# A decoder layer with seven-product projections: loads and operand splits moved to other places, row loads tied behind operand loads, the first MLP block loaded apart

## The chip, the cores and the metric

The kernel runs on one core of a Trainium2 chip. The metric is the device time of one execution in microseconds (us), and the median of several runs is compared. The core has five engines that the profile names: PE (TensorE, the matmuls, with PEld for its weight loads), DVE (VectorE), ACT (ScalarE), POOL (GpSimd) and SP (SyncE, which here only issues DMAs). ACT and POOL issue DMAs too, each in its own queue, between their other instructions.

## The reference

One decoder layer over 1024 tokens of width 1024, all in float32:

```python
u = x * (1.0 + sc1) + sh1
proj = u @ w_in
y_a = _sliding_window_attention(qa, ka, va, sinks) @ w_oa
y_b = _gated_deltanet(dq, dk, dv, z, b_raw, a_raw, ...) @ w_ob
mixed = (sigmoid(g_a) * y_a + sigmoid(g_b) * y_b) @ w_out
x = _layer_norm(ALPHA * x + (1.0 + gt1) * mixed, ln1_g, ln1_b)
u2 = x * (1.0 + sc2) + sh2
h = square(relu(u2 @ w_ff1 + b_ff1))
x = _layer_norm(ALPHA * x + (1.0 + gt2) * (h @ w_ff2 + b_ff2), ln2_g, ln2_b)
```

The shifts, scales and gates (`sh1`, `sc1`, `gt1` and so on) come from a small product of the conditioning vector with `w_ada`. `w_ff1` is 1024 x 4096 and `w_ff2` 4096 x 1024.

## The kernel before

**Operands.** Each float32 operand of a large product is split into a high part (a copy on ACT, line 212) and a low part (a subtraction on DVE, line 213), and each product is made of three matmuls: high by high, high by low, low by high. `split_s` issues the ACT copy at once and the DVE subtraction some places later.

**Seven products.** The projections `w_oa`, `w_ob`, `w_ff1` and `w_ff2` are each done as a 2 x 2 block product in seven block products instead of eight, so that sums and differences of blocks are operands. Their names in the code are 11, 21, 22, T1, T2, T3 and T4; m is the number of the product.

**Order by hand.** PE, DVE and ACT run in an order that is written out. `count` is the number of matmuls issued so far, and `at(p, f)` lets `f` issue its instructions when `count` reaches p; p is called a place here. Since each engine runs its own list in order, a place fixes only which instruction stands before which on one engine: an engine may run ahead of PE, and stands where an instruction of its own must wait. DMAs that ACT issues stand in its list as well (`ga_load`, `ta_load`, `sg_load`). SP and POOL are not ordered by hand: a planner orders their DMAs, and each goes out when the buffer it writes is free and its data is there.

**Stages from 915 us on**, where the change lies:

- OA is the place of the first output projection (`y_a`, stage 0 in the loop whose matmul is line 1684), OB = OA + 336 that of the second (`y_b`, stage 1). Each has two groups of 168 places, 12 places to a product. In one part of a group, products 1, 6, 7 and 4 add into the same PSUM bank one after the other, and between two of them the bank is read: by a copy on ACT (`o_part`, line 1614) or by an add on DVE (`o_full`, line 1433). In the other part, products 5 and 3 share a bank in the same way. The first product 1 of stage 1 stands at OB+72 and 84 (two column blocks), product 6 at OB+96 and 108; the adds between are placed at OB+85 and 97.
- The operands of stage 0 are partly in SBUF (11, T2, T3, T4 are split by `q_part`) and partly loaded: `q_load` and `q2_load` bring T1, 21, 22 and then all seven of stage 1 into the three `or` buffers, and `q_split` and `q2_split` split them at the places in `RSPLIT` and `RSPLIT2`, two halves to a name. A load is let go by the low part of the split three halves before it. The first three go out at `CLOSE` = OA+26, when the memory of the stage before is free, whose last user is `gz`, the evacuation of the last gate unit, and its DMA to `gb_d` (lines 1396 and 1397). Weights for the products are loaded as `owr` and split as `wo`.
- `ga_load` and `ga_act` load and squash the gates of `y_a`, `ta_load` loads the gated `y_a` back in stage 1, `sg_load` and `sg_act` (line 1633) do the same for the gates of `y_b`; `o_gate` (line 1618) writes the gated `y_a` to `ta_d`, and `y_out` (lines 1637, 1638) forms the sum. `ga` and `ta` share two `gate` buffers.
- `hd_out` writes the last head's output; its inner `more` makes the negative (`neg`, line 1373), writes it to DRAM and lets POOL add it into the stored sums T2, T3 and T4 by accumulating DMAs.
- E0 = OB + 336 begins the mix (`w_out`, line 1900), four segments of SEG = 96 places, with the layer norm and its transposes between (`u2_turn`, line 1771, `pair_turn`, line 1820, `t_split`). Its weights and the first five blocks of `w_ff1` come through the two `wr` buffers (`w_go`, `w_more`); `w_first` splits the first block, `W0`, at E0+330.
- F0 = E0 + 384 begins the first MLP matmul (line 2271; `f_load`, `f_beta`, `f_gamma`), G0 the last product (line 2331). There `s_load` brings two operands of 512 KB for every 24 places, the first two steps from ACT's queue, the rest from SP's. `rows_load` brings six row vectors, each spread over all 128 partitions (512 KB), placed at G0+62 and every 24 places after; `rr_load` brings the residual, placed at G0+200 and every 60.

Of the kernel before, what the change touches and what calls it, by code (L numbers as in the profile page):

```python
# [9 lines left out]
F32 = mybir.dt.float32  # L10
F32R = mybir.dt.float32r
# [23 lines left out]
def hybrid_layer_kernel(ctx: ExitStack, tc: tile.TileContext,  # L35
# [122 lines left out]
    for q in (0, 1, 0):  # L158
        for kq in range(4):
            later.append((w_out[kq * Q:(kq + 1) * Q, q * HALF:(q + 1) * HALF].rearrange("(k p) c -> p k c", p=P),  # L160
                         [P, 2, HALF]))
    later += [in_cols(w_ff1, i * P) for i in range(EARLY)]
    ready, raws = [], []
    AHEAD = 2

# [1191 lines left out]
    def hd_out(h, half):  # L1357
        d = heads[h]
        assert ("o", h) in flags
        tp = psum("b", 2)  # L1360
        for j in range(4):
            T.transpose(tp[:, chunk(j)], o_chunk(d, 4 * half + j), ident)

        def put():
            V.scalar_tensor_tensor(out=d["sz"][:, halves[half]], in0=tp, scalar=normw, in1=d["sz"][:, halves[half]],
                                   op0=ALU.mult, op1=ALU.mult)
            r, k, o = d["sz"][:, halves[half]], h % 4, oq_d
            if h == 7 and half == 0:
                d["vr"] = gpool.tile([P, S], F32, tag="gate", name="neg")
            neg = d["vr"][:, halves[half]]  # L1370

            def more():
                A.activation(out=neg, in_=r, func=AF.Copy, scale=-1.0)
                if h < 4 and half == 1:
                    nc.sync.dma_start(out=o["T3"][k], in_=neg)
                    for name, src in (("T1", neg), ("T4", neg), ("T2", d["vr"][:, halves[0]])):
                        nc.gpsimd.dma_start(out=o[name][k], in_=src, accum_op=ALU.add)
                elif h >= 4:
                    if h == 7:
                        nc.sync.dma_start(out=nq_d[half], in_=neg)  # L1380
                    src = nq_d[half] if h == 7 else neg
                    for name, src in ((("T4", src),), (("T3", o["22"][k]), ("T2", src), ("T4", o["22"][k])))[half]:
                        nc.gpsimd.dma_start(out=o[name][k], in_=src, accum_op=ALU.add, max_dma_last_dim=HALF)

            for name in (("11", "T1", "T4"), ("T2",))[half] if h < 4 else (("21", "22")[half],):
                nc.sync.dma_start(out=o[name][k], in_=r)
            act(4, 2.7, more)
        now("V", 2, 3.3, put)

    def gb_done(i):  # L1390
# [125 lines left out]

    REST = [(n, j) for n in ("T1", "21", "22") for j in range(2)]
    OB = OA + 336
    RSPLIT = (70, 76, 94, 100, 116, 124)
    ORDER2 = ("11", "T1", "21", "22", "T2", "T3", "T4")  # L1520
    HOME2 = {"11": (1, 6), "21": (1, 0), "T1": (1, 2), "22": (1, 4), "T2": (0, 0), "T3": (0, 2), "T4": (0, 4)}
    REST2 = [(n, j) for n in ORDER2 for j in range(2)]
    RSPLIT2 = (150, 160, 196, 206, 220, 230, 316, 340, 348, 358, 372, 384, 398, 412)

    for kind, h in units_h:
        if kind == "q":
# [123 lines left out]
        after(6, lambda: V.scalar_tensor_tensor(out=lo, in0=y, scalar=-1.0, in1=hi.bitcast(F32),  # L1650
                                                op0=ALU.mult, op1=ALU.subtract))

    for p, q, g, c in ((30, 80, 0, 3), (60, 100, 0, 0), (136, 166, 0, 2), (160, 190, 0, 1), (190, 226, 1, 0),
                       (210, 246, 1, 1), (278, 306, 1, 3), (302, 332, 1, 2)):
        at(OA + p, ga_load, g, c)
        at(OA + q, ga_act, g, c)
    for p, g, c in ((-8, 0, 0), (18, 0, 1), (108, 0, 3), (134, 0, 2), (190, 1, 2), (192, 1, 0), (275, 1, 3), (322, 1, 1)):
        at(OB + p, ta_load, g, c)
    for p, q, f in ((10, 50, 0), (12, 62, 1), (14, 90, 4), (16, 100, 5), (200, 240, 6), (202, 248, 7), (204, 260, 2), (206, 270, 3)):
        at(OB + p, sg_load, f)  # L1660
        at(OB + q, sg_act, f)
    for p, f, half in ((218, 0, None), (224, 1, None), (258, 6, 0), (266, 4, None), (274, 5, None), (290, 7, 0),
# [139 lines left out]
    def u2_rest(j, p):  # L1802

        at(p, t_one, j)
        at(p + 1, quad_split, j, "22", 1, 1)
        at(p + 8, t_sums, j)
        for kh in range(2):
            for k in range(4):
                at(p + 12 + 3 * (4 * kh + k), t_split, j, kh, k)

    rawp = {}

# [67 lines left out]

    W0 = []

    def w_first():
        raw = raws.pop(0)[0]
        for kh in range(2):
            W0.append([pe.tile([P, 4, P], F32R, tag="t", name="w0", bufs=8) for _ in "hl"])
            split_s(W0[kh][0], W0[kh][1], raw[:, 4 * kh:4 * kh + 4, :], 5)

    w_more()
    for p in [1, 13] + [SEG * s + o for s in (0, 2) for o in (61, 73, 86, 98)] + [3 * SEG + o for o in (42, 98, 118, 134, 154)]:  # L1890
        at(E0 + p, w_first if p == 3 * SEG + 42 else w_go)
        at(E0 + p + 8, w_more)

    def mix_mm(pt, tok, c):

# [155 lines left out]
    at(F0 + 1, f_load, 0)  # L2051
    at(F0 + 32, f_sums, 0, V)
    at(F0 + 33, f_sums2, 0, V)
    at(F0 + 92, f_beta, 0)
    at(F0 + 100, f_gamma, 0)
    at(pos[0, 5] + 10, f_delta, 0)
    for i in range(1, NPAIR):
        if i < EARLY:
# [69 lines left out]
    def s_load(s):  # L2128
# [7 lines left out]
            src = w_ff2[(r0 + f) * P:(r0 + f + 2) * P, halves[c0]].rearrange("(f p) c -> p f c", p=P)  # L2136
        else:
            src = wt_d[{5: 0, 6: 1, 7: 2, 4: 3}[m], f:f + 2].rearrange("f p c -> p f c")
        q.dma_start(out=b, in_=src)

    def s_split(s, j):
        hi, lo = stp[s, j] = [s_tile(w, F32R, "sp") for w in PARTS[place(s)][2 * j:2 * j + 2]]
# [13 lines left out]
    def rows_load(n):  # L2156
        name, src = ROWS[n]
        rows_[name] = wp.tile([P, D], F32, tag="wl" if n % 2 else "wh", name=name)
        row(rows_[name], src, nc.sync)

    def rows_sums():
        G2, B2 = rows_["G2"], rows_["B2"]
# [3 lines left out]

    def rr_load(t):
        rr[t] = big.tile([P, D], F32, tag=f"{'hl'[t // 4]}{4 + t % 4}", name="rr")
        nc.sync.dma_start(out=rr[t], in_=res_d[SLOTS[t]])

    def res_sums(t, i):
        r = rr[t]
# [237 lines left out]
```

## Time and profile before

| | |
|---|---|
| median of three runs | 1798.21 us (1798.05 to 1801.23) |
| the profiled execution | 1799.15 us |
| its span, first to last instruction | 1797.4 us |
| mean granted TensorE clock | 0.997 |

The span by stage, with what PE and the DMA engines did:

| stage | span, us | PE busy, us | DMA share | GB/s |
|---|---|---|---|---|
| all before the projections | 0 to 915 | 909.41 | 0.74 | 198 |
| first output projection | 915 to 996 | 78.17 | 0.97 | 316 |
| second output projection | 996 to 1079 | 78.66 | 0.64 | 225 |
| mix | 1079 to 1174 | 93.61 | 0.43 | 149 |
| first MLP matmul | 1174 to 1482 | 307.52 | 0.82 | 279 |
| last product | 1482 to 1797 | 305.96 | 0.63 | 216 |

How to read the rows that follow: a row of a timeline has the start and the length in us, the engine (with q: its sequencer, which issues a DMA), the line, the operation, what it writes and reads, the shape and the count; in square brackets stands how long the engine was idle before it and what ended that. PE's matmuls are pipelined, so that a matmul is shown longer than the distance to the next one.

### The profile page before, as it was taken

How to read it: one execution, taken by the hardware profiler on the slowest of the kernel's cores; microseconds unless marked ns; L12 is line 12 of the kernel's file. 1: busy time of each engine (PE TensorE's matmuls, PEld its weight loads, DVE VectorE, ACT ScalarE, POOL GpSimd, SP SyncE). 2: the span in 40 equal slices, each digit the busy share in tenths (PEclk: the TensorE clock that was granted, in tenths of full speed). 3: DMA queues.
4: the chain of work that ended last, by engine and by line, in shares of the span. 5: the costliest groups of instructions: out<-in, count | busy, mean ns of one | idle time of the engine just before them, and what ended most of it. 6: DMA issues, size and time to landing. Idle time of an engine off the chain costs nothing.

```text
span 1797.4 us, 26402 instructions
## 1 busy us (share of the span) xinstructions
PE 1773.3 (99%) x9086; PEld 1491.4 (83%) x9086; DVE 1316.5 (73%) x2391; ACT 1055.7 (59%) x2373; POOL 367.6 (20%) x495
## 2 busy tenths in 40 slices
PE   9999999999999999999999999999999999999998
PEld 6888888888888888888887788788888888888887
DVE  7689588988855576766657666888777765676697
ACT  4689578887874565665565542475555554434341
POOL 0334235665531011122111000002122210000000
PEclk9999999999999999999999999999999999999999
DMA  9557945687786687877889754369888889655671
GB/s 330 163 204 266 287 141 133 119 182 133 144 243 197 154 211 212 222 210 200 237 236 342 271 188 164 129 190 320 306 276 272 285 296 384 228 196 182 207 258 48
DMA packets 287305, 393.85 MB, mean 219 GB/s; under 512 B 27994, under 2 KB 180259, under 8 KB 286915
## 3 DMA queue, kind: packets, MB, share of 16 engines
q1 hardware_dynamic: 219282, 245.95, 42.6%
q0 software_dynamic: 51856, 112.62, 24.3%
q10 hardware_dynamic: 16032, 33.59, 5.3%
q8 instruction: 72, 1.18, 0.3%
q14 instruction: 63, 0.51, 0.1%
HBM read 273.86 MB, written 141.83 MB: 231 GB/s over the span
## 4 chain that ended last, share of the span: by engine, by line
PE 83%; DMA 5%; DVE 5%; ACT 3%; issue 1%; POOL 0%; ACTq 0%; DVEq 0%; SPq 0%; POOLq 0%
PE mm L255 30%; PE mm L2271 8%; PE mm L2331 6%; PE a L2331 4%; PE b L2331 4%; PE b L2271 4%; PE mm L1684 4%; PE a L2271 3%; PE c L2331 2%; PE c L939 2%; PE mm L183 1%; PE mm L185 1%; PE mm L184 1%; PE b L1684 1%; PE a L864 1%
## 5 line engine op out<-in xcount | busy, mean ns | idle before, releaser
L255 PE MATMUL mm<-uh,wh 128*128 128x512 f32 x800 | 319.6, 400 | 0.0
L255 PE MATMUL mm<-uh,wl 128*128 128x512 f32 x800 | 319.4, 399 | 0.0
L255 PE MATMUL mm<-ul,wh 128*128 128x512 f32 x800 | 318.8, 398 | 0.0
L213 DVE TENSOR_TENSOR sp<-sraw,sp 128x1024 fp32r<-128x1024 f32 x112 | 132.7, 1220 | 77.0 <-ACT sp L212 77.0
L212 ACT ACTIVATE sp<-sraw 128x1024 fp32r<-128x1024 f32 x112 | 112.6, 1054 | 121.9 <-PE b L2331 75.3
L255 PEld LDWEIGHTS mm<-uh,wh 128*128 128x128 f32 x800 | 150.7, 188 | 26.2
L255 PEld LDWEIGHTS mm<-uh,wl 128*128 128x128 f32 x800 | 150.8, 189 | 26.1
L255 PEld LDWEIGHTS mm<-ul,wh 128*128 128x128 f32 x800 | 150.8, 188 | 26.1
L2331 PE MATMUL mm<-sp 128*128 128x512 f32 x528 | 136.2, 389 | 1.0 <-DVE sp L213 1.0
L2331 PEld LDWEIGHTS mm<-sp 128*128 128x128 f32 x528 | 98.7, 188 | 21.7 <-DVE sp L213 1.5
L2331 PE MATMUL a<-sp 128*128 128x512 f32 x336 | 92.3, 389 | 0.0
L1309 ACT ACTIVATE vn<-a,brk 128x128 f32<-128x128 f32 x64 | 23.6, 369 | 110.4 <-PE a L1307 110.4
L1684 PE MATMUL mm<-qh,wo 128*128 128x512 f32 x256 | 81.3, 395 | 4.9 <-ACT sg L1633 4.3
L871 DVE CUSTOM_DVE_ANT_0 nscore<-a,amask,nsink 128x256 f32<-128x256 f32 (+1 forms) x128 | 54.4, 462 | 40.8 <-PE a L864 40.5
L2331 PE MATMUL b<-sp 128*128 128x512 f32 (+1 forms) x336 | 79.7, 374 | 0.0
L882 POOL TENSOR_TENSOR sm<-sm 128x256 f32<-128x256 f32 x56 | 56.6, 1011 | 93.7 <-ACT sm L878 68.3
L2331 PEld LDWEIGHTS a<-sp 128*128 128x128 f32 x336 | 63.1, 188 | 13.1
L2331 PEld LDWEIGHTS b<-sp 128*128 128x128 f32 x336 | 60.3, 188 | 11.2
L230 DVE TENSOR_TENSOR wl<-wr,wh 128x1024 fp32r<-128x1024 f32 x48 | 62.7, 1306 | 6.1 <-ACT wh L226 5.9
L213 DVE TENSOR_TENSOR wl<-fraw,wh 128x1024 fp32r<-128x1024 f32 x43 | 52.5, 1221 | 15.9 <-ACT wh L212 15.9
L212 ACT ACTIVATE wh<-fraw 128x1024 fp32r<-128x1024 f32 x43 | 45.0, 1056 | 32.0 <-PE b L2271 27.0
L1684 PEld LDWEIGHTS mm<-qh,wo 128*128 128x128 f32 x256 | 48.9, 191 | 16.4 <-ACT sg L1633 4.7
(562 smaller groups left out, 4782.8 us busy)
## 6 DMA issues: line engine op xcount, KB each, us to landing
wr<-in_w_in_dram SPq DMA_DIRECT2D x60, 512.0 KB, 4.6
sraw<-hf_d SPq DMA_DIRECT2D x54, 512.0 KB, 4.4
adaw<-in_w_ada_dram SPq DMA_DIRECT2D x83, 256.0 KB, 5.1
fraw<-in_w_ff_dram SPq DMA_DIRECT2D x32, 512.0 KB, 5.7
sraw<-wt_d SPq DMA_DIRECT2D x32, 512.0 KB, 4.3
hf_d<-t ACTq DMA_DIRECT2D x48, 256.0 KB, 5.2
wt_d<-wx POOLq DMA_DIRECT2D x48, 256.0 KB, 3.1
sraw<-in_w_ff_dram SPq DMA_DIRECT2D x22, 512.0 KB, 5.4
```

The costliest lines, as they stand in the source:

```text
L183: T.matmul(t, lhsT=wh[:, k, :], rhs=xh[k][:, sl], start=k == 0, stop=False)
L212: A.activation(out=hi, in_=src, func=AF.Copy)
L213: after(lag, lambda: V.tensor_tensor(out=lo, in0=src, in1=hi.bitcast(F32), op=ALU.subtract))
L230: V.tensor_tensor(out=hl[1], in0=raw, in1=hl[0].bitcast(F32), op=ALU.subtract)
L255: T.matmul(ts[half], lhsT=w[:, k, :], rhs=xx[k][:, sl], start=k == 0 and m == 0, stop=k == KT - 1 and m == 2)
L871: V.tensor_tensor_reduce(out=ns[:, i, 1:1 + W], in0=sc[:, i * 2 * P:i * 2 * P + W], in1=amask[:, mo:mo + W], scale=-1.0, scalar=nsink[:, 2 ...
L882: behind["join"] = G.tensor_tensor(out=sm[:, :, 1 + P:1 + 2 * P], in0=sm[:, :, 1:1 + P], in1=sm[:, :, 1 + P:1 + 2 * P], op=ALU.add).ins
L939: T.matmul(av[:, 0:256], lhsT=vt[:, b, :], rhs=p_[:, m, :], start=p_ is full and m == 0, stop=p_ is prods[-1][1] and m == 1)
L1309: after(1, lambda: A.activation(out=vn, in_=Wp[:, 0:P], func=AF.Copy, scale=brk[:, n, h:h + 1]))
L1684: T.matmul(pt, lhsT=lw[:, k, own], rhs=r[:, k % 2, :], start=begin and k == 0 and x_ == 0, stop=k == 3 and x_ == 2, skip_group_check=True)
L2271: T.matmul(pt, lhsT=a[:, kk, :], rhs=b[k], start=begin and k == 0 and x_ == 0, stop=k == 3 and x_ == 2, skip_group_check=True)
L2331: T.matmul(to, lhsT=a[:, f, t * P:(t + 1) * P], rhs=b[:, f, lo:up], start=(begin or own) and s % NS == 0 and f == 0 and x_ == 0, stop=s % ...
```

## The change

It has five parts. (1) In `hd_out`, for the last head, `more` goes to OA+28 and OA+34 instead of the place right behind its source. (2) In the two output projections, the places of the operand splits (`RSPLIT`, `RSPLIT2`) and of the loads and sigmoids of `ga`, `ta` and `sg` are other ones. (3) The first block of `w_ff1` no longer goes through the `wr` buffers but is loaded in two halves into tiles of its own (tag `t`, which the mix's evacuation uses too) at E0+254 and 258 and split at E0+310 and 314; `t_split` comes six places later. (4) `f_beta` and `f_gamma` of the first pair go from F0+92 and 100 to 78 and 97. (5) In the last product, each `rows_load` and `rr_load` is tied on SP's queue behind the last `s_load` placed before it. What is computed does not change.

```diff
-    later += [in_cols(w_ff1, i * P) for i in range(EARLY)]
+    later += [in_cols(w_ff1, i * P) for i in range(1, EARLY)]
...
-            act(4, 2.7, more)
+            if h == 7:
+                at(OA + (28, 34)[half], more)
+            else:
+                act(4, 2.7, more)
...
-    RSPLIT = (70, 76, 94, 100, 116, 124)
+    RSPLIT = (62, 68, 86, 100, 112, 126)
...
-    RSPLIT2 = (150, 160, 196, 206, 220, 230, 316, 340, 348, 358, 372, 384, 398, 412)
+    RSPLIT2 = (150, 160, 196, 206, 220, 230, 262, 286, 316, 328, 344, 356, 372, 388)
...
-    for p, q, g, c in ((30, 80, 0, 3), (60, 100, 0, 0), (136, 166, 0, 2), (160, 190, 0, 1), (190, 226, 1, 0),
+    for p, q, g, c in ((50, 92, 0, 3), (75, 108, 0, 0), (136, 166, 0, 2), (160, 190, 0, 1), (190, 226, 1, 0),
                        (210, 246, 1, 1), (278, 306, 1, 3), (302, 332, 1, 2)):
         at(OA + p, ga_load, g, c)
         at(OA + q, ga_act, g, c)
-    for p, g, c in ((-8, 0, 0), (18, 0, 1), (108, 0, 3), (134, 0, 2), (190, 1, 2), (192, 1, 0), (275, 1, 3), (322, 1, 1)):
+    for p, g, c in ((36, 0, 0), (60, 0, 1), (108, 0, 3), (134, 0, 2), (190, 1, 2), (192, 1, 0), (275, 1, 3), (322, 1, 1)):
         at(OB + p, ta_load, g, c)
-    for p, q, f in ((10, 50, 0), (12, 62, 1), (14, 90, 4), (16, 100, 5), (200, 240, 6), (202, 248, 7), (204, 260, 2), (206, 270, 3)):
+    for p, q, f in ((10, 52, 0), (24, 66, 1), (72, 120, 4), (86, 132, 5), (200, 240, 6), (206, 248, 7), (218, 262, 2), (228, 274, 3)):
         at(OB + p, sg_load, f)
         at(OB + q, sg_act, f)
...
-                at(p + 12 + 3 * (4 * kh + k), t_split, j, kh, k)
+                at(p + 18 + 3 * (4 * kh + k), t_split, j, kh, k)
...
-    def w_first():
-        raw = raws.pop(0)[0]
-        for kh in range(2):
-            W0.append([pe.tile([P, 4, P], F32R, tag="t", name="w0", bufs=8) for _ in "hl"])
-            split_s(W0[kh][0], W0[kh][1], raw[:, 4 * kh:4 * kh + 4, :], 5)
+    w0raw = []
+    def w_first_load(kh):
+        w0raw.append(pe.tile([P, 4, P], F32, tag="t", name="w0r", bufs=8))
+        nc.sync.dma_start(out=w0raw[kh], in_=in_cols(w_ff1, 0)[0][:, 4 * kh:4 * kh + 4, :])
+    def w_first(kh):
+        W0.append([pe.tile([P, 4, P], F32R, tag="t", name="w0", bufs=8) for _ in "hl"])
+        split_s(W0[kh][0], W0[kh][1], w0raw[kh], 5)
...
+    for kh in range(2):
+        at(E0 + 2 * SEG + 62 + 4 * kh, w_first_load, kh)
+        at(E0 + 3 * SEG + 22 + 4 * kh, w_first, kh)
...
-    at(F0 + 92, f_beta, 0)
-    at(F0 + 100, f_gamma, 0)
+    at(F0 + 78, f_beta, 0)
+    at(F0 + 97, f_gamma, 0)
...
-        q.dma_start(out=b, in_=src)
+        behind["s"] = q.dma_start(out=b, in_=src).ins
...
-        row(rows_[name], src, nc.sync)
+        with tc.issue_after(behind["s"]):
+            row(rows_[name], src, nc.sync)
...
-        nc.sync.dma_start(out=rr[t], in_=res_d[SLOTS[t]])
+        with tc.issue_after(behind["s"]):
+            nc.sync.dma_start(out=rr[t], in_=res_d[SLOTS[t]])
```

More of the change, by code (lines that the diff above doesn't have):

```diff
@@ L1881, in hybrid_layer_kernel @@
     W0 = []
-    def w_first():
-        raw = raws.pop(0)[0]
-        for kh in range(2):
-            W0.append([pe.tile([P, 4, P], F32R, tag="t", name="w0", bufs=8) for _ in "hl"])
-            split_s(W0[kh][0], W0[kh][1], raw[:, 4 * kh:4 * kh + 4, :], 5)
+    w0raw = []
[5 more added lines that the diff above has]
+        split_s(W0[kh][0], W0[kh][1], w0raw[kh], 5)
     w_more()
-    for p in [1, 13] + [SEG * s + o for s in (0, 2) for o in (61, 73, 86, 98)] + [3 * SEG + o for o in (42, 98, 118, 134, 154)]:
-        at(E0 + p, w_first if p == 3 * SEG + 42 else w_go)
+    for p in [1, 13] + [SEG * s + o for s in (0, 2) for o in (61, 73, 86, 98)] + [3 * SEG + o for o in (98, 118, 134, 154)]:
+        at(E0 + p, w_go)
         at(E0 + p + 8, w_more)
+    for kh in range(2):
+        at(E0 + 2 * SEG + 62 + 4 * kh, w_first_load, kh)
+        at(E0 + 3 * SEG + 22 + 4 * kh, w_first, kh)
     def mix_mm(pt, tok, c):
```

## The prediction

> **What bounds the kernel now.** I read the page first, then who waited for whom on PE, then PE's timeline around each wait, then ACT, DVE and SP at those places.
>
> ```profile
> span 1797.4 us, 26402 instructions
> PE 1773.3 (99%) x9086; PEld 1491.4 (83%) x9086; DVE 1316.5 (73%) x2391; ACT 1055.7 (59%) x2373; POOL 367.6 (20%) x495
> ```
>
> The profiled execution took 1799.15 us, its span 1797.4, so 1.75 lie around it; the median of the runs, 1798.21, is 0.94 below it. PE is the bound: only its waits can be won. They are few:
>
> ```profile
> PE mm L1684 <- ACT sg L1633: 4.3, 1, 4.3
> PE b L1684 <- DVE t L1433: 1.2, 1, 1.2
> PE mm L2331 <- DVE sp L213: 1.0, 1, 1.0
> PE b L1820 <- DVE r L1760: 0.5, 1, 0.5
> PE b L1820 <- DVE st L1759: 0.5, 1, 0.5
> PE c L2271 <- DVE wl L213: 0.3, 1, 0.3
> ```
>
> The columns are total us, times, longest. All six lie where the diff edits: the two output projections (L1684), the mix and its turns (L1820), the first MLP matmul (L2271), the last one (L2331). A wait costs more than its idle time, as PE's timeline shows:
>
> ```profile
> 1007.57 0.39 PE L1684 MATMUL b<-qh,wo 128*128 128x512 f32 x1
> ...
> 1013.01 0.39 PE L1684 MATMUL mm<-qh,wo 128*128 128x512 f32 x1
> ...
> 1018.22 0.39 PE L1684 MATMUL mm<-qh,wo 128*128 128x512 f32 x1
> 1022.95 0.74 PE L1684 MATMUL mm<-qh,wo 128*128 128x512 f32 x1 [4.34 <-ACT sg L1633]
> ...
> 1026.44 0.40 PE L1684 MATMUL mm<-qh,wo 128*128 128x512 f32 x1
> ```
>
> Between 1007.57 and 1013.01 lie two products of 12, so a matmul, and so a place in the hand-written order, is 5.44 / 24 = 0.227 us. From 1018.22 to 1022.95 are 4.73, of which 4.50 are lost. The eight matmuls from 1022.95 to 1026.44 then take 3.49 where 8 x 0.227 = 1.81 would do: 1.7 more. This wait costs **6.2**.
>
> ```profile
> 1000.00:1015.00 15.00, 15.00 (x68) 12.43 (x67) 4.86 (x5) 5.55 (x8) 0.00 (x0) 1.00 1.04 410
> 1015.00:1025.00 10.00, 5.66 (x21) 4.36 (x21) 7.43 (x8) 9.73 (x12) 0.00 (x0) 0.90 0.28 95
> ```
>
> The last three columns are granted clock, DMA share and GB/s. After the long idle the clock falls below 1.00: those are the slow eight. The Trainium skill (TensorE: Matmul & The Clock Gate, Part 1) says the clock halves after an idle window of about 3.4 us and stays so for about as long; the row agrees at 4.34 idle. By that rule a new wait of some 3.4 costs 1.7 more too; by the row alone only one as long as 4.34 does.
>
> Why does PE wait? The name in the row (the sigmoid of a gate) is only what came last on ACT:
>
> ```profile
> 1001.01 7.14 SPq L1541 DMA_DIRECT2D or<-oqT_d  x2
> ```
> ```profile
> 1013.70 1.07 ACT L212 ACTIVATE qh<-or 128x1024 fp32r<-128x1024 f32 x1 [3.62 <-DMA or<-oqT_d]
> ```
> ```profile
> 1020.98 1.23 DVE L213 TENSOR_TENSOR ql<-or,qh 128x1024 fp32r<-128x1024 f32 x1 [1.15 <-ACT qh L212]
> 1022.12 0.68 DVE L1433 TENSOR_TENSOR t<-t,mm 128x512 f32<-128x512 f32 x1
> ```
>
> An operand load issued at 1001.01 lands at 1013.7, 12.7 later, because from 1000 to 1015 the DMA engines are full (share 1.04, 410 GB/s): four 512 KB `sg` loads, two `ta`, the operand loads and the weights are all out at once. ACT stands 3.62 behind it, then is 97% busy (9.73 of 10.00), and DVE stands behind ACT. The add at 1022.12 reads the bank that the first product of OB+72 filled; the product at OB+96 adds into that bank and may not start before it. It ends at 1022.80, and PE starts at 1022.95. So this is a landing, paid three queues later.
>
> **The change part by part.** For the smaller waits I count idle + 0.16 (0.39 of modelled matmul less 0.227) + 0.11 (the next one shows 0.50 instead of 0.39).
>
> *Second projection (stage 1).* The splits of 22, T2, T3 and T4 come 54 to 24 places earlier (T4's second from OB+76 to OB+52), so nothing that waits for an operand load stands ahead of the add at OB+85 within 28 places (6.4 us). Two of four `sg` loads (1 MB) leave the full stretch for OB+72 and 86, and both `ta` loads go to OB+36 and 60. On ACT the last operand split is at OB+52 instead of 76, so no landing can hold what follows. The full 15 us moved 410 x 15 = 6.2 MB; without 1 MB of `sg` and the earlier operand loads it has some 4.7, well under what 15 us hold. I take **6.0** of 6.2 (bounds 0 to 6.2). Cover: the moved splits go into OA+253 to 345, where DVE has room:
>
> ```profile
> 973.10:994.20 21.10, 21.10 (x95) 17.46 (x94) 15.98 (x20) 11.56 (x13) 3.26 (x6) 1.00 0.94 324
> ```
>
> DVE is busy 15.98 of 21.1; two more low parts make 15.98 + 2 x 1.23 = 18.4, and ACT 11.56 + 3 x 1.06 = 14.7. If that cover fails, each late add delays PE directly; I charge 0.3 (0 to 1).
>
> *First projection (stage 0).*
>
> ```profile
> 917.74 0.63 ACT L1373 ACTIVATE neg<-sz 128x512 f32<-128x512 f32 x1 [0.65 <-DVE sz L1365]
> 918.28 0.62 ACT L212 ACTIVATE qh<-ts 128x512 fp32r<-128x512 f32 x1
> 918.80 0.58 ACT L1396 ACTIVATE gz<-mm 128x512 f32<-128x512 f32 x1
> ```
> ```profile
> 919.43 0.50 PE L1684 MATMUL mm<-qh,wo 128*128 128x512 f32 x1 [0.50 <-ACT gz L1396]
> ```
>
> PE waits 0.50 (cost 0.77) for a bank that `gz` empties, and `gz` stands behind `neg` with its 0.65 wait. With `neg` at OA+28 and 34, `gz` ends about 1.2 earlier, before PE asks: **0.77** won. What moves with it: two copies, two writes on SP, four accumulating DMAs on POOL; behind them on POOL are only `ta_d` writes (first at OA+112), and T2 is not loaded before OA+231. ACT takes them where it later idles 3.27 (next fence).
>
> ```profile
> 946.84 0.50 PE L1684 MATMUL a<-ql,wo 128*128 128x512 f32 x1 [0.67 <-DVE ql L213]
> ```
> ```profile
> 952.93 0.50 PE L1684 MATMUL b<-ql,wo 128*128 128x512 f32 x1 [0.36 <-DVE ql L213]
> ```
> ```profile
> 958.33 0.50 PE L1684 MATMUL b<-qh,wo 128*128 128x512 f32 x1 [1.24 <-DVE t L1433]
> ```
>
> These cost 0.94 + 0.63 + 1.51 = 3.08. All hang on operands that land late:
>
> ```profile
> 926.63 0.89 SPq L1473 DMA_DIRECT2D or<-at_d  x2
> ```
> ```profile
> 925.00:935.00 10.00, 10.00 (x46) 8.28 (x45) 2.46 (x3) 3.70 (x6) 2.04 (x2) 1.00 1.15 315
> ```
> ```profile
> 934.51 1.06 ACT L212 ACTIVATE qh<-or 128x1024 fp32r<-128x1024 f32 x1 [3.27 <-DMA or<-at_d]
> 935.48 0.58 ACT L1614 ACTIVATE t<-mm 128x512 f32<-128x512 f32 x1
> 936.52 1.06 ACT L212 ACTIVATE qh<-or 128x1024 fp32r<-128x1024 f32 x1 [0.47 <-DMA or<-at_d]
> ```
>
> The first operand loads go out at 926.63, when the second `gb_d` write frees their memory; that write follows `gz`, so they go some 1.2 earlier, and the two `ga` loads and the accumulations go later: about 2 to 4 us earlier landing in a stretch of share 1.15. The splits, 8 places earlier, can follow. I take two thirds, **2.0** (bounds -3.0, rival A, to 3.08).
>
> *Mix and turns.*
>
> ```profile
> 1159.77 1.16 ACT L212 ACTIVATE w<-wr 128x512 fp32r<-128x512 f32 x2 [4.51 <-DMA wr<-in_w_ff_dram]
> ```
> ```profile
> 1160.44 1.30 DVE L213 TENSOR_TENSOR w<-wr,w 128x512 fp32r<-128x512 f32 x2 [1.86 <-ACT w L212]
> 1161.65 0.68 DVE L1748 TENSOR_TENSOR tm<-mm,gt 128x512 f32<-128x512 f32 x1
> ```
>
> The first MLP block lands late, and its low parts push the mix's evacuation to 1161.65, which ends 1.2 later than it could; this comes out at the turns as the two waits of 0.5. Loaded 56 places (12.7 us) ahead of its split, it lies in DVE's 1.86 gap. I take **1.1** (0 to 1.3). The six-place shift of `t_split` and the freed weight buffers I put at 0 (-0.6 to 0.4): they change the order among short ACT and DVE steps, beside a `mm` stage with no wait there above 0.5.
>
> *First MLP.* `f_beta` 14 places earlier, for the row of 0.3 (cost 0.57). ACT only runs the same work in another order: **0.3** (-0.5 to 0.6).
>
> *Last product.*
>
> ```profile
> 1472.50 0.33 SPq L1704 DMA_DIRECT2D lb<-in_ln_b_dram  x1
> ```
> ```profile
> 1470.00:1495.00 25.00, 23.96 (x106) 19.54 (x105) 13.46 (x17) 14.80 (x19) 2.18 (x4) 1.00 1.04 403
> ```
> ```profile
> 1494.44 0.73 PE L2331 MATMUL mm<-sp 128*128 128x512 f32 x2 [1.04 <-DVE sp L213]
> ```
>
> SP is not ordered by hand, and row loads meant for G0+62 and after (`lb` is the fourth) went out before G0 (1482), ahead of the operands, into a full 25 us. Each is 512 KB, so four are 2 MB / 403 GB/s = 5 us. Tied behind the loads of their place, they let the first operands land up to 5 us earlier, where 1.31 is lost (1.04 + 0.27): **1.2** (0 to 1.3). What waits for them: `rows_sums` 56 places after `lb`, `res_sums` 50 places after each `rr`, 11 us or more.
>
> The second half's `sg` loads (OB+206 to 228) keep 34 places to their sigmoids and meet no PE wait: 0.
>
> **Sum.** 6.0 + 0.77 + 2.0 + 1.1 + 0.3 + 1.2 = 11.4, less 0.3 for DVE and 0.5 for new small waits = 10.6. The profiled 1799.15 becomes 1788.5, the median 1798.2 becomes **1787.6**. All waits gone: 6.2 + 0.77 + 3.08 + 1.3 + 0.6 + 1.3 = 13.3, or 1785; I go to 1784 for the waits not listed.
>
> **The rivals.**
>
> ```profile
> 935.66 0.95 PE L1684 MATMUL mm<-qh,wo 128*128 128x512 f32 x2
> ```
>
> A. *A new wait at OA+84.* Both T1 splits (62, 68) now stand ahead of the copy at 73, which was between them and which the product at OA+84 waits for. If T1 lands as before, the copy ends at 936.52 + 1.06 + 0.58 = 938.2, while PE is there at 935.1 (the last matmul before it starts at 935.66 in the row above, plus 0.23, less the 0.77 of `gz`): 3.0 lost, after which the later operands are in time, so stage 0 wins 0.8 in all and the sum is 0.8 + 6.0 + 1.1 + 0.3 + 1.2 - 0.8 = 8.6: 1789.6, or 1791 if the clock falls as it does after 1022.95. Against it: the earlier issue. PE does not wait if T1's second half lands 3.0 earlier, by 933.5.
>
> B. *Stage 1 only shrinks.* The operand loads still have about 35 places (7.9 us) between being let go and their split, and one took 12.7. If half of the 4.5 stays: 1790; with a lower clock too: 1792.
>
> C. *Slower.* The gate loads come later, so they can land too late. `ta` at OB+36 is read by DVE at OB+86: 50 places, 11.3 us; the add behind it at OB+97 has 11 places, 2.5 us, to spare. So from a landing of 13.9 us on PE waits, and the same holds for `ta` at 60 and `sg` at 72 and 86. Four such waits eat 10.6 from landings of 16.5 on; at 18 they cost 4 x 4.1 and the time is 1804. The operand load above took 12.7, in the full stretch; 1015 to 1025, where two of these loads go, has a share of 0.28. The Trainium skill (DMA: Bandwidth & Descriptors, Rules for kernel authors) speaks for this rival: issue a DMA early and wait for it late. The 12.7 speaks against it: early loads delayed the urgent one.
>
> D. *It does not do what it says.* Operand loads leave when a buffer is freed, not at their place; if landings stay as they are, only `gz` and the MLP block remain: 0.77 + 1.1 = 1.9, or 1796.3.
>
> **How the numbers follow.** Forecast 0.60, A 0.13, B 0.12, D 0.09, C 0.06. A, B and the forecast's bounds span 1784 to 1794, and leave out C and D. Over 0.2% (3.6 us, about what a measurement here can tell) faster: 0.60 + 0.13 + 0.12 = 0.85; within: D, 0.09; slower: C, 0.06.
>
> **What would show it.** Right: no PE wait above 1 at OB+96, clock 1.00 there; no wait for `gz` at OA+12; first MLP block split before the mix's evacuation; rows issued after G0 and no wait at G0+48. A would show as a PE wait on ACT at OA+84; B as `qh` still waiting for `or` just before OB+85; C as DVE waiting for `ta` or ACT for `sg`. Wrong altogether if the long wait goes and the time does not follow.

## The result and the profile after

The kernel after takes **1788.92 us** (median of four runs, 1787.79 to 1789.64), the kernel before, run beside it, 1799.34 (1798.05 to 1801.23). The ratio is 0.9941, with a 95% interval of 0.9923 to 0.9958. So 10.4 us are gone, between 7.6 and 13.9 by the interval's ends; the prediction had 10.6. The profiled execution of the kernel after took 1789.64, its span 1787.6.

Its page, and then the waits of PE that are left from 915 us on (total us, times, longest):

```profile
span 1787.6 us, 26397 instructions
PE 1769.3 (99%) x9086; PEld 1490.3 (83%) x9086; DVE 1315.5 (74%) x2391; ACT 1054.3 (59%) x2373; POOL 369.7 (21%) x495
```
```profile
PE b L1687 <- DVE t L1436: 1.2, 1, 1.2
PE mm L1911 <- DVE wl L213: 1.1, 2, 0.6
PE c L2284 <- ACT t L1996: 0.8, 1, 0.8
PE b L1687 <- DVE ql L213: 0.8, 1, 0.8
```

PE's idle time has fallen from 24.1 us (1797.4 less 1773.3) to 18.3, its busy time, in which slow matmuls count, by 4.0. The wait of 4.3 and those at the transposes (line 1820, now 1823) and in the last product (2331, now 2344) are gone. What is left from 915 us on lies in the first projection (line 1687, before 1684), the mix (1911) and the first MLP matmul (2284). The two windows around OB+96, with granted clock, DMA share and GB/s at the end, and DVE at the add that made PE wait before:

```profile
1000.00:1015.00 15.00, 15.00 (x67) 12.40 (x67) 6.39 (x6) 9.51 (x12) 0.00 (x0) 1.00 0.99 356
1015.00:1025.00 10.00, 10.00 (x46) 8.28 (x45) 9.61 (x14) 4.13 (x4) 0.00 (x0) 1.00 0.50 160
```
```profile
1014.53 0.69 DVE L1436 TENSOR_TENSOR t<-t,mm 128x512 f32<-128x512 f32 x1 [3.47 <-PE mm L1687]
```

The DMA engines are still almost full (0.99), but now DVE waits 3.47 for PE there and not PE for DVE, and the clock stays at 1.00. In the first projection:

```profile
917.49 0.57 ACT L1399 ACTIVATE gz<-mm 128x512 f32<-128x512 f32 x1
...
922.58 0.63 ACT L1373 ACTIVATE neg<-sz 128x512 f32<-128x512 f32 x1
...
930.32 2.00 ACT L212 ACTIVATE qh<-or 128x1024 fp32r<-128x1024 f32 x2
932.55 0.60 ACT L1617 ACTIVATE t<-mm 128x512 f32<-128x512 f32 x1 [0.23 <-PE mm L1687]
936.34 0.37 ACTq L1606 DMA_DIRECT2D ga<-ga_d  x1
938.10 1.06 ACT L212 ACTIVATE wo<-owr 128x1024 fp32r<-128x1024 f32 x1 [4.95 <-DMA owr<-wsa_d]
```

`gz` no longer stands behind `neg`, and both halves of T1 are split at 930.32 without a wait (before: 934.51 and 936.52). Then ACT stands 4.95 us. In the first part of it the second `ga` load holds ACT's queue and goes out only at 936.34; a weight load that is in at 938.1 ends it. With this the ground that was won is lost again: PE waits for the low part of 22 and for an add.

```profile
951.49 0.50 PE L1687 MATMUL b<-ql,wo 128*128 128x512 f32 x1 [0.76 <-DVE ql L213]
956.88 0.50 PE L1687 MATMUL b<-qh,wo 128*128 128x512 f32 x1 [1.20 <-DVE t L1436]
```

In the last product the row loads now leave between the operand loads, after G0 (1473.7); the fourth, `lb`, left at 1472.50, ahead of G0 (1482), before:

```profile
1487.95 0.46 SPq L1707 DMA_DIRECT2D gt<-gt_d  x1
...
1496.11 0.34 SPq L1707 DMA_DIRECT2D lb<-in_ln_b_dram  x1
```

### The profile page after: what moved, and what is told of

Read it like the earlier page. It is cut to its first block, busy times and chain, and to the rows that moved or that the text cites. A ratio compares the mean times of both kernels' runs of the same rounds, so it can differ in the third digit from the quotient of the medians.

```text
span 1787.6 us, 26397 instructions
## 1 busy us (share of the span) xinstructions
PE 1769.3 (99%) x9086; PEld 1490.3 (83%) x9086; DVE 1315.5 (74%) x2391; ACT 1054.3 (59%) x2373; POOL 369.7 (21%) x495
## 3 DMA queue, kind: packets, MB, share of 16 engines
q1 hardware_dynamic: 219298, 245.95, 42.8%
## 4 chain that ended last, share of the span: by engine, by line
PE 87%; DMA 4%; DVE 4%; ACT 3%; issue 1%; POOL 0%; SPq 0%; ACTq 0%; DVEq 0%; POOLq 0%
PE mm L255 30%; PE mm L2284 8%; PE mm L2344 7%; PE a L2344 4%; PE b L2284 4%; PE mm L1687 4%; PE b L2344 4%; PE a L2284 3%; PE c L2344 2%; PE b L1687 2%; PE c L939 1%; PE mm L1911 1%; DMA t_d<-tc 1%; PE a L1687 1%; PE mm L183 1%
## 5 line engine op out<-in xcount | busy, mean ns | idle before, releaser
L924 POOL TENSOR_SCALAR_AFFINE_SELECT pl<-ph 128x512 fp32r<-128x512 f32 x56 | 59.2, 1058 | 17.3 <-DVE ph L917 17.2
```

Source lines behind the costliest of these rows:

```text
L924: G.affine_select(out=flat4(part), in_=flat4(full), pattern=[[0, 4], [1 if odd else -1, P]], compare_op=ALU.is_ge if odd else ALU.is_gt, f ...
```

## The experiments

To see where time goes, I cut each trace by the start of PE's first matmul in each stage, so that every lost microsecond falls into one cell. All kernels of the study in one table (us; the columns after the first are from start to start, the last one to the end of the last matmul, and the tail of 8.4 behind it is left out; in brackets the experiment, whose edit can shift line numbers by some):

| kernel | start of OA | stage 0, group 0 | group 1 | stage 1, group 0 | group 1 | mix | first MLP | last product |
|---|---|---|---|---|---|---|---|---|
| before | 915.58 | 42.75 | 38.36 | 44.29 | 38.08 | 95.21 | 307.87 | 306.87 |
| after | 915.55 | 41.33 | 38.40 | 38.08 | 38.08 | 94.46 | 307.81 | 305.53 |
| splits alone (1) | 914.70 | 42.20 | 38.38 | 38.08 | 38.24 | 95.80 | 307.86 | 306.06 |
| gate loads alone (2) | 914.28 | 43.23 | 38.38 | 38.78 | 38.08 | 95.23 | 307.85 | 306.28 |
| after, old splits, no ties (3) | 914.60 | 41.83 | 38.36 | 38.08 | 38.08 | 94.46 | 307.89 | 306.68 |
| after, old gate loads, old block (4) | 916.68 | 41.06 | 39.68 | 38.36 | 38.08 | 95.37 | 307.85 | 305.53 |
| after, old negative, old beta (5) | 916.29 | 41.12 | 38.37 | 38.08 | 38.08 | 94.61 | 307.85 | 305.53 |
| after, old `ga`, old `t_split` (6) | 914.36 | 46.35 | 38.08 | 38.08 | 38.08 | 94.36 | 307.85 | 305.53 |
| after, old first splits (7) | 915.18 | 44.22 | 38.38 | 38.08 | 38.08 | 94.63 | 307.87 | 305.53 |
| after, accumulations late (8) | 913.92 | 38.55 | 48.09 | 38.08 | 38.08 | 93.45 | 307.88 | 305.53 |
| after, accumulations spread (9) | 913.89 | 38.55 | 41.14 | 38.08 | 38.08 | 93.44 | 307.87 | 305.53 |
| after, two accumulations late (10) | 914.21 | 40.17 | 41.48 | 38.08 | 38.08 | 93.66 | 307.45 | 305.53 |
| combined (11) | 913.97 | 38.55 | 39.67 | 38.08 | 38.08 | 93.47 | 307.41 | 305.53 |
| after again (12) | 913.62 | 41.95 | 39.80 | 38.08 | 38.08 | 94.38 | 307.89 | 305.53 |

168 places of 0.2267 us are 38.08: the second projection now runs without any loss, and the last product repeats to 0.01 wherever its loads are tied. The first projection varies between runs of the same code: before, 1 and 2 have the old one and take 81.11, 80.58 and 81.61 for both groups; after, 3 and 12 have the new one and take 79.73, 80.19 and 81.75. So I read nothing from less than 2 us there. One trace stands behind each row; each edit is read in its own stage.

My theory at the start: the long wait was a landing paid late, and the place of the split ahead of the add decides, not the bytes. The rival: the gate loads' bytes decide.

**1. The splits alone.** The kernel before with one line of the change:

```diff
-    RSPLIT2 = (150, 160, 196, 206, 220, 230, 316, 340, 348, 358, 372, 384, 398, 412)
+    RSPLIT2 = (150, 160, 196, 206, 220, 230, 262, 286, 316, 328, 344, 356, 372, 388)
```

> The kernel before with one edit: the operand splits of the second projection at their new places (the second list, RSPLIT2). Judged by stage 1, from its first matmul to the first of the mix: 82.4 us before, 76.2 after the whole change. My theory (a landing paid three queues later; it is the place of the split, ahead of the add, that decides): the 4.7 us gap before OB+96 goes or falls under 1 us, though the four gate loads still leave together; the clock stays at 1.00 and stage 1 takes 76 to 78. Rival 1 (the gate loads fill the DMA engines, and only fewer bytes help): the operand load still lands 12 us after its issue, ACT stands behind it, and at least half of the gap stays: stage 1 at 79 to 82. Rival 2 (both are needed, as in the prediction's B): some 79.

Measured: stage 1 takes 76.32 instead of 82.37; the gap at OB+96 is gone altogether. Its SP and ACT:

```profile
994.14 0.36 SPq L1541 DMA_DIRECT2D or<-oqT_d  x1
...
998.74 0.36 SPq L1541 DMA_DIRECT2D or<-oqT_d  x1
```
```profile
1003.71 1.06 ACT L212 ACTIVATE qh<-or 128x1024 fp32r<-128x1024 f32 x1 [4.90 <-DMA owr<-wsb_d]
...
1011.22 1.06 ACT L212 ACTIVATE qh<-or 128x1024 fp32r<-128x1024 f32 x1 [0.81 <-DMA or<-oqT_d]
1013.01 1.06 ACT L212 ACTIVATE wo<-owr 128x1024 fp32r<-128x1024 f32 x1 [0.73 <-DMA owr<-wsb_d]
1013.97 0.58 ACT L1614 ACTIVATE t<-b 128x512 f32<-128x512 f32 x1
```

The load that took 12.7 us before was that of T3's second half. Here it goes out at 994.14 instead of 1001.01, 5.5 us earlier when both are counted from the start of stage 1 (995.28 and 996.69), and its split is at 1003.71 instead of 1013.70. ACT still stands 4.90 us there, but the add is far off. The load of T4's second half, the last one, takes 12.5 us (998.74 to 1011.2), and ACT waits for it only 0.81. So a load in this stretch can still take as long as before, but each is asked for earlier, as the theory has it.

**2. The gate loads alone.** The kernel before with the new places of `ta_load`, `sg_load` and `sg_act`.

```diff
-    for p, g, c in ((-8, 0, 0), (18, 0, 1), (108, 0, 3), ...
+    for p, g, c in ((36, 0, 0), (60, 0, 1), (108, 0, 3), ...
-    for p, q, f in ((10, 50, 0), (12, 62, 1), (14, 90, 4), (16, 100, 5), ...
+    for p, q, f in ((10, 52, 0), (24, 66, 1), (72, 120, 4), (86, 132, 5), ...
```

> The kernel before with one edit: the ta and sg loads of the second projection, and the sigmoids behind them, at their new places; the operand splits where they were. My theory (the place of the split decides): the splits of T3 and T4 still stand ahead of the add at OB+85, but the operand load that took 12.7 us lands faster without 1 MB of sg beside it, some 9 us; the gap before OB+96 falls from 4.7 to between 0.5 and 3 us, so stage 1 at 77 to 80.5. Rival 1 (the bytes alone are the cause): the gap goes wholly, 76.2. Rival 2 (only the places of the splits count): 82.

Measured: 38.78 + 38.08 = 76.86, so 5.5 of the 6.2 go by this alone, more than my theory allowed (77 to 80.5).

```profile
1000.22 1.79 SPq L1541 DMA_DIRECT2D or<-oqT_d  x2
```
```profile
1008.13 1.06 ACT L212 ACTIVATE qh<-or 128x1024 fp32r<-128x1024 f32 x1 [1.03 <-DMA or<-oqT_d]
```

With the `ta` loads and two of the four `sg` loads out of its way, T3's second half takes 7.9 us (1000.22 to 1008.1) instead of 12.7, and even splits at the late places are almost in time (0.7 is left). Neither the theory nor the rival alone is right: each of the two edits is enough, and they do not add up.

**3. and 4. The complements.** The kernel after with the old `RSPLIT2` and without the two `tc.issue_after(behind["s"])` (3), and with the old gate loads of stage 1, the old `w_first` and `t_split` at `p + 12` (4).

> The kernel after with two parts undone, in two different stages: the operand splits of the second projection back at their old places, and the row and residual loads of the last product no longer tied behind its operand loads. Stage 1: it has the gate loads of the changed kernel and the splits of the old one, so what the gate-loads-alone run gives, 77 to 80.5 by my theory, 76.2 by the rival that bytes alone decide. Last product: my theory has the 1.43 us gap at G0+48 back, 306.9 instead of 305.5, with row loads issued before G0; the rival, that the better order in the first MLP matmul or other moves gave the 1.3, leaves it at 305.5.

> The kernel after with two parts undone, in two different stages: the ta and sg loads of the second projection (and their sigmoids) back at their old places, and the first MLP block again through the two wr buffers and split at E0+330, with t_split at its old six places earlier. Stage 1: 76 to 78 by my theory that the place of the split decides, 79 to 82 by the rival that the gate loads' bytes decide. Mix: 95.2 instead of 94.5 by my theory, with the waits of 0.5 us before the transposes back and a gap of 1 us gone at E0+133 or E0+313 if those new waits come from the new order; the rival, that the 0.75 came from t_split's shift, is not told apart from it here but from the place of the gaps: the transposes at E0+361 belong to the block, E0+236 to t_split.

Measured in stage 1: 76.16 without the new splits, 76.44 without the new gate loads. This confirms 1 and 2 from the other side; my 77 to 80.5 for kernel 3 was wrong. The last product without ties takes 306.68, and the rows leave early again:

```profile
1463.07 0.33 SPq L1707 DMA_DIRECT2D B<-in_b_ff_dram  x1
1465.51 0.33 SPq L1707 DMA_DIRECT2D lb<-in_ln_b_dram  x1
```

The four untied kernels take 306.87, 306.06, 306.28 and 306.68 (mean 306.47), all ten tied ones 305.53: the ties are worth 0.94, and 1.34 only against the one trace that I predicted from. The mix of kernel 4 takes 95.37: the block of its own is worth 0.9 (the four kernels with the old block have a mean of 95.40, the six with the new one and the old evacuation 94.48). Its 39.68 in stage 0, group 1 is not shown to be an effect of the edit: the unchanged kernel shows 39.80 in run 12, with PE's wait at the same place, OA+324.

**5. The negative back at its old place**, and `f_beta`, `f_gamma` of the first pair too.

```diff
-            if h == 7:
-                at(OA + (28, 34)[half], more)
-            else:
-                act(4, 2.7, more)
+            act(4, 2.7, more)
...
-    at(F0 + 78, f_beta, 0)
-    at(F0 + 97, f_gamma, 0)
+    at(F0 + 92, f_beta, 0)
+    at(F0 + 100, f_gamma, 0)
```

> The kernel after with two parts undone, in two stages: in the first projection the negative of the last head, its write and its accumulating DMAs back right behind their source; in the first MLP matmul the f_beta and f_gamma of the first pair back at F0+92 and 100. Stage 0: my theory (moving the negative lets gz run at once, and with it the gb_d write and the first operand loads) has the gap of 0.9 us at OA+12 back and the first operand load issued some 1.5 to 2 us later, 926 to 927 instead of 924.7, so a first group of 42.0 to 42.8 us instead of 41.3. The rival (the earlier loads come from the gate loads' move) has the OA+12 gap back and nothing else: 42.0, with the loads no later than 925.5. First MLP matmul: the gap at F0+144 falls from 1.15 to 0.6 and one of 0.64 at F0+122 comes back, so no net difference (307.8 to 307.9) if the move only exchanges two waits.

Measured: 41.12, not 42 to 42.8. The wait for `gz` is back, but the one at OA+151 (0.76 idle in the kernel after) is gone, although the first operand loads go out 1.7 us later after OA:

```profile
920.15 0.50 PE L1684 MATMUL mm<-qh,wo 128*128 128x512 f32 x1 [0.51 <-ACT gz L1396]
957.42 0.50 PE L1684 MATMUL b<-qh,wo 128*128 128x512 f32 x1 [1.24 <-DVE t L1433]
```

So in these traces moving the negative exchanges one wait for another, which the theory and the rival both missed. The first MLP matmul takes 307.85 by the old places and 307.81 by the new: an exchange too.

**6. The first two `ga` loads back at OA+30 and 60**, and `t_split` at `p + 12`.

```diff
-    for p, q, g, c in ((50, 92, 0, 3), (75, 108, 0, 0), (136, ...
+    for p, q, g, c in ((30, 80, 0, 3), (60, 100, 0, 0), (136, ...
```

> The kernel after with two parts undone, in two stages: the first two ga loads (and their sigmoids) of the first projection back at OA+30 and 60, and t_split six places earlier in the mix. Stage 0: if the gate loads' bytes delay the weight load that ACT stood 4.95 us for, that wait grows and the first group takes 42 to 43; if they do not, it stays at 41.3 plus or minus 0.3, which is what I expect more, since the load of two MB moves by only 20 and 15 places inside the same full stretch. Mix: if the 0.75 came from the first MLP block alone, the mix stays at 94.5 and the gap at E0+313 keeps its 0.93; if the shift of t_split made that gap, the gap goes back to 0.34 and the mix takes 93.9; if t_split's shift cured the 0.65 at E0+236, that gap is back and the mix takes 95.0.

Measured: 46.35, where I expected 41.3 (and the two loads are 512 KB each, so 1 MB and not two). ACT and PE:

```profile
935.46 0.37 ACTq L1606 DMA_DIRECT2D ga<-ga_d  x1
935.88 0.60 ACT L1617 ACTIVATE t<-mm 128x512 f32<-128x512 f32 x1 [8.42 <-DMA nq_d<-neg]
```
```profile
936.53 0.79 PE L1687 MATMUL mm<-qh,wo 128*128 128x512 f32 x1 [5.21 <-ACT t L1617]
```

`neg` lies in a `gate` buffer, which the second `ga` load takes next. Issued from ACT, that load must wait until `neg` has been written to DRAM (the write of the second half went out at 925.02, and the `ga` load follows at 935.46), and ACT's whole queue stands behind it for 8.42 us, the copy that PE needs among it. So the `ga` loads had to move because the negative moved. In the mix, the gap of 0.93 at E0+313 goes and one of 0.65 at E0+236 comes (94.36): `t_split`'s shift is an exchange.

**7. The first splits back** (`RSPLIT = (70, 76, 94, 100, 116, 124)`).

> The kernel after with one part undone: the operand splits of the first projection at their old places (RSPLIT). My theory: the splits of T1 at 70 and 76 run later on ACT than at 62 and 68, the loads behind them are let go later, and the waits at OA+127, 151 and 168 add up to at least 3 us again, so a first group of 42.0 to 42.8. The rival (in this stage the landing decides, not the place: ACT stands 4.95 us for a weight load anyway): the first group stays at 41.3 plus or minus 0.3.

Measured: 44.22, outside both ranges.

```profile
936.32 1.06 ACT L212 ACTIVATE qh<-or 128x1024 fp32r<-128x1024 f32 x1 [3.55 <-DMA nq_d<-neg]
...
951.65 1.06 ACT L212 ACTIVATE qh<-or 128x1024 fp32r<-128x1024 f32 x1 [6.13 <-DMA or<-attn_d]
```
```profile
952.75 0.50 PE L1687 MATMUL b<-qh,wo 128*128 128x512 f32 x1 [2.85 <-ACT qh L212]
```

It is again the place that decides, but by another way than I thought: the second half of T1, at OA+76, now stands behind the `ga` load of OA+75, which waits for `neg`'s write. At 62 and 68 both halves are ahead of it.

**8. The accumulations late.** In the kernel after, ACT's 4.95 us stand in a stretch whose DMA engines are over-full. Here the four accumulating DMAs go behind the first writes of the gated `y_a`; besides, the evacuation of the mix's fourth tile is later, and `f_beta` is at F0+86.

```diff
+                        at(OA + (150, 156)[half], accs)
...
+                            with tc.issue_after(behind["ta"]):
                                 nc.gpsimd.dma_start(out=o[name][k], in_=src, accum_op=ALU.add, max_dma_last_dim=HALF)
...
-                lag = {(2, 6): 14, (2, 7): 56, (3, 7): 10}.get((s, t), 1)
+                lag = {(0, 3): 9, (2, 6): 14, (2, 7): 56, (3, 7): 10}.get((s, t), 1)
```

> The kernel after with three additions, in three stages. Stage 0: the last head's four accumulating DMAs wait on POOL behind the first writes of the gated y_a (OA+150). My theory of the waits that are left at OA+151 and 168 (1.26 and 1.59 between starts): the DMA engines are full from 923 to 947, the weight load lands 11.3 us after its issue, ACT stands 4.95 us for it, and all that follows is late; with the accumulations out of that stretch the weight load lands 3 to 5 us earlier, both gaps fall under 0.6 and the first group takes 38.8 to 39.8 instead of 41.3. The rival (DVE, busy without a pause from 945 to 960, sets the pace): the load lands earlier, the group stays within 0.5 of 41.3. A second rival: the accumulations only move the full stretch, and new waits come in the second group, 38.4 now. Mix: the evacuation of its fourth tile eight places later, behind the low part of a weight block; the gap of 0.98 at E0+133 goes, 93.7 instead of 94.5. First MLP matmul: f_beta of the first pair at F0+86, between the old 92 and the new 78; if ACT's 2.57 us stand for its source is what pushes the copy before F0+144, that gap falls from 1.15 to about 0.6 and none comes back at F0+122: 307.3; else 307.8.

Measured: group 0 takes 38.55, all but 0.5 of its loss gone, so DVE did not set the pace there; but group 1 takes 48.09, as the second rival had it. ACT in group 0, then POOL and ACT in group 1:

```profile
933.27 1.06 ACT L212 ACTIVATE wo<-owr 128x1024 fp32r<-128x1024 f32 x1 [1.76 <-DMA owr<-wsa_d]
```
```profile
951.93 1.89 POOL L1390 DMA_DIRECT2D oqT_d<-nq_d  x1
962.15 1.01 POOL L1390 DMA_DIRECT2D oqT_d<-oq_d  x1 [8.34 <-DMA oqT_d<-nq_d]
962.78 2.57 POOL L1631 DMA_DIRECT2D ta_d<-t  x4
```
```profile
971.57 0.60 ACT L1626 ACTIVATE t<-b 128x512 f32<-128x512 f32 x1 [9.78 <-DMA ta_d<-t]
```

Counted from the start of OA, ACT's long wait for the weight load ends 3.2 earlier (19.4 us after it instead of 22.6), and the second `ga` load does not hold ACT before it. But the second accumulation into T4 must wait for the first, POOL's queue stands 8.34 behind it with the `ta_d` writes, and ACT needs a buffer that one of these frees. The mix falls to 93.45 and the wait at E0+133 is gone, as in kernels 9 to 11 with the same edit: it came from the order on DVE. `f_beta` at 86 changes nothing (307.88).

**9. and 10. Fewer of them late, one at a time.** In 9, T4's first stays early, T2, T3 and T4's second go behind the writes before OA+150, 204 and 250 (`t_split` at `p + 15`). In 10, only T2 and T4's second go late (176, 236), and `f_delta` goes from `pos[0, 5] + 10` to `+ 14`.

> The kernel after with three additions. Stage 0: of the last head's four accumulating DMAs the first (T4) stays where it is; T2, T3 and the second into T4 go out one at a time, tied on POOL behind the write of the gated y_a before OA+150, 204 and 250. In the run with all four behind OA+150 the first group took 38.55 us, but the second 48.09 instead of 38.4, where POOL's queue stood 8.3 us for the first accumulation into T4 and ACT then 9.8 us for a write of the gated y_a behind it. My theory (the burst and the pair into T4 did that, not the accumulations as such): the first group at 38.6 to 39.8 and the second at 38.1 to 39.5, 76.7 to 79 in all against 79.7 after. The rival (the DMA engines have no room for them anywhere between 945 and 995, share 0.94 to 1.05): the second group at 41 or more, or stage 1 above 78. Mix, with the fourth tile's evacuation later (93.45 in that run) and t_split 15 instead of 18 places behind its sums: 92.8 to 93.5 if the gap of 0.84 at E0+313 goes as it did at 12, 93.5 to 94.1 if the one of 0.65 at E0+236 comes instead.

> The kernel after with three additions. Stage 0: only T2 and the second accumulation into T4 go late (tied behind the writes before OA+176 and 236); T4's first and T3's go out at once. My theory (two accumulations before 930 disturb little, as they landed within 7 us where the negative was at its old place): the first group at 38.8 to 40.2, the second at 38.1 to 39.0. The rival (no room late): the second group at 40 or more. The second rival (T3's alone is enough to delay the weight load): the first group at 41 to 41.6. Mix, with the fourth tile's evacuation later and t_split as in the kernel after: 93.45 as in the run before. First MLP matmul: the split of the first difference (f_delta) four places later, behind the copy that the product at F0+144 waits for; if that split on ACT is what makes the gap of 1.16 there, it falls to 0.6 and the stage takes 307.3; the rival (the copy is late for other ACT work) leaves it at 307.8.

Measured: both groups together 79.69 and 81.65, against 79.73 and 81.75 in the two traces of the kernel after. What group 0 wins, group 1 gives back, as the rival of no room had it, though group 1 of the unchanged kernel also varies between 38.4 and 39.8. What sets these runs apart is where PE waits in group 1: in 9, 10 and 11 there is a wait at OA+264 that no kernel with the accumulations early shows. In 9, two of the three still left together:

```profile
962.98 2.17 POOL L1385 DMA_DIRECT2D oqT_d<-oq_d  x2
```

The mix of 9 takes 93.44 with `t_split` between its two places, as 8 does with the new one. `f_delta` four places later makes the first MLP matmul 307.45 instead of 307.81, its wait 0.26 instead of 0.77: that split stood ahead of the copy.

**11. and 12. Combined, and the kernel after again.** 11 has the two small gains, T4's first accumulation early, and T2, T3 and T4's second behind the writes before OA+150, 204 and 318. Five rounds, both beside the same runs of the kernel before.

> The kernel after with what helped: the fourth tile's evacuation later in the mix (93.45 us instead of 94.46) and f_delta four places later (307.45 instead of 307.81), and the last head's accumulations into T2, T3 and, the second, T4 tied behind the writes before OA+150, 204 and 318. In the run with the last at 250 both T3's and T4's went out together at 963, behind the same write, and the second group took 41.14, where the first had won 2.8. If that pair made the 2.7, the second group takes 38.1 to 39.5 with T4's accumulation alone at some 980, and the time is 4 us below the kernel after. The rival (the DMA engines have no room in 945 to 1000 whatever the order) has the 2.7 stay in the second group or come out in stage 1: then only 1.4 are won against the kernel after, about 0.08%.

> The kernel after once more, unchanged, beside the one above, on the same chip and against the same runs of the kernel before. Stages by start to start as in its first trace (first projection 79.7, second 76.2, mix 94.5, first MLP matmul 307.8, last product 305.5), with the first group of the first projection the only one that I expect to differ by over 0.3, since the group of the kernel before took 42.2 to 43.2 in different runs. Ratio to the kernel before 0.993 to 0.996.

Measured: combined 1787.76 us (1785.04 to 1788.13), ratio to before 0.9931 (0.9918 to 0.9943); after again 1789.87 (1788.89 to 1791.24), ratio 0.9948 (0.9934 to 0.9961). In run 12 group 1 of the first projection differs by 1.4 from the first trace, which I had not expected; the rest repeats. All five of the one lie below all five of the other, and the medians differ by 2.1 us, not the 4 that I hoped for, of which mix and first MLP matmul make 1.4 by the traces. Its group 1 (39.67) lies between theory and rival. It is no longer than in run 12 (39.80), but the wait is another one: 1.1 us at OA+264 in the combined kernel, 1.2 at OA+324 in run 12. So accumulations that leave 925 to 945 still cost something later. That stretch in the kernel after, and in the combined one:

```profile
925.00:945.00 20.00, 20.00 (x90) 16.46 (x89) 7.91 (x8) 11.82 (x14) 3.04 (x3) 1.00 1.12 304
```
```profile
925.00:945.00 20.00, 20.00 (x90) 16.57 (x89) 11.43 (x12) 14.57 (x16) 1.31 (x2) 1.00 1.04 348
```

POOL issues fewer DMAs, the engines move more bytes (348 against 304 GB/s), and DVE and ACT get more done.

## Why the prediction was right, and which terms were not

- **Second projection, 6.0 of 6.2: right** (6.21 between the two traces), and the clock did stay at 1.00. The argument named both the earlier places and the freed bytes as one chain. The runs show two sufficient causes: places alone win 6.05 with a load of 12.5 us still in the stretch, loads alone 5.5. One step was off without harm: the stretch was to hold some 4.7 MB and no longer be full, but it moved 356 GB/s x 15 us = 5.3 MB at a share of 0.99.
- **First projection, 0.77 + 2.0: wrong.** The means of three traces each are 81.10 before and 80.56 after: 0.5, less than the spread. The step that failed is "The splits, 8 places earlier, can follow. I take two thirds, 2.0". T1 landed and was split early, as said; then ACT stood 4.95 us for a weight load in the same over-full stretch, and 22 was late again. The `gz` wait went, but kernel 5 shows that its 0.77 came back at OA+151. Kernel 8 shows what else lay in that stretch: with the four accumulations late, group 0 loses 0.5 instead of 3.25 (and group 1 more). The prediction looked only at what stands behind them on POOL. I also did not see that `neg` holds a `gate` buffer: that the moved negative holds up the `ga` loads on ACT was named in no term, and kernels 6 and 7 show that it costs 5 and 3 us where the `ga` loads or T1's splits do not move with it.
- **Mix, 1.1: the mechanism right, the size 0.9.** The block's high parts ran at 1147.91 and the two waits of 0.5 are gone; the wait at E0+133, which kernels 1 and 2 with the old block show too, grew from 0.51 to 0.98 between starts. `t_split`'s 0 was right: an exchange.
- **First MLP matmul, 0.3: wrong, 0.** `f_beta` cures F0+122, and the wait at F0+144 grows by as much.
- **Last product, 1.2: right**, 1.34 between the two traces, 0.94 on the mean.
- **The deductions, 0.3 + 0.5**, paid for part of the first projection's failure. That 10.6 came so near to 10.4 is therefore in part luck. By the means, 6.2 + 0.5 + 0.9 + 0.9 = 8.5, where the medians give 10.4 and, in run 12, 9.8. The rest is not assigned: the earlier stages end between 913.6 and 916.7 in these traces, and the long wait itself was traced only once.
- **The rivals.** A did not come: T1's halves ran without a wait, ahead of the copy. B did not: no operand load holds the add, and the clock is 1.00. D is out. C did not come by the way described, no `ta` or `sg` is late in the kernel after; its nearest kin, a load that holds ACT's queue, cost 5 us in kernel 6. The rule of the Trainium skill that spoke for C (DMA: Bandwidth & Descriptors, Rules for kernel authors: issue early, wait late) is borne out here only in part: in kernel 1 the operand loads did go out earlier, but the waits for them were put earlier too, to places with room before the add, and that won 6.05. In kernel 2 two `sg` loads went out 58 and 70 places later and two `ta` loads 44 and 42, and that won 5.5 with none of them late.

## What to carry to other kernels

Where a late transfer stops an engine, look for two cures, another place for the instruction that waits and fewer bytes beside the transfer, and try each alone: here either was enough. A DMA issued from a compute engine's queue waits there for its buffer and holds everything behind it (ACT 8.42 us in kernel 6), so when a tile is moved, find who takes its buffer next and from which queue. In a stretch whose DMA engines are full, moving transfers can only move the wait, as in kernels 8 to 10; count both sides of the move.

## What the runs showed of the hardware

Three things I had not expected. First, the clock falls after less idle time than the 4.34 us that the prediction went by. In kernel 7, 2.85 us idle, one matmul and 0.76 idle were enough:

```profile
954.01 0.79 PE L1687 MATMUL b<-ql,wo 128*128 128x512 f32 x1 [0.76 <-DVE ql L213]
```
```profile
948.00:953.00 5.00, 2.15 (x10) 1.44 (x8) 1.14 (x3) 1.35 (x2) 0.56 (x1) 1.00 1.04 403
953.00:960.00 7.00, 6.24 (x21) 4.66 (x21) 6.97 (x9) 4.66 (x5) 1.08 (x2) 0.76 0.84 262
```

The granted clock is 0.76 from 953 to 960. The wait of 0.76 alone, at 951.49 in the kernel after, left it at 1.00 there (950 to 955). After 5.21 idle in kernel 6 it is 0.55 from 936 to 942. The Trainium skill (TensorE: Matmul & The Clock Gate, Part 1) gives a window of about 3.4 us: neither idle stretch of kernel 7 reaches it alone, both with the matmul between make some 4.

Second, accumulating DMAs go with a DMA share above 1 at a low rate (1.12 at 304 GB/s from 925 to 945 in the kernel after, against 1.04 at 410 from 1000 to 1015 in the kernel before). Third, in such a stretch even the short write of `neg`'s second half (128 x 512, 256 KB) held back what waited for it for 10.4 us (from its issue at 925.02 to 935.46 in kernel 6).
